# Low parts of the down projection's weights: from VectorE to ScalarE and an adding transfer

## The chip, the core and the metric

The kernel runs on one core of one Trainium2 chip. The metric is the device time of one execution in microseconds; runs of the same kernel are compared by their median.

## The reference, cut to what matters

One layer of a decoder with two token mixers (a gated delta rule and a retention) side by side, a gated sum of the two, an output projection, and then a SwiGLU block, all in float32, for 256 tokens of width 2048. What the change touches is the last product of the SwiGLU block:

```python
hn = rmsnorm(h, norm2_w[l])
h = h + (jax.nn.silu(hn @ w_gate[l]) * (hn @ w_up[l])) @ w_down[l]
return rmsnorm(h, norm_f_w)
```

`w_down` is 5632 x 2048 (46.1 MB).

## The kernel before

Each float32 product is made of three passes on TensorE with operands in a rounded float32 form: the high part of the weights times the high and the low part of the tokens, and the low part of the weights times the high part of the tokens. The kernel works through a row of **units** of weights of up to 1 MB. For each unit, SyncE's queue loads the weights from HBM into a buffer `raw` (`fetch_next`, line 150). ScalarE rounds them to the high part `hi` (line 163), VectorE subtracts, `lo = raw - hi` (line 164), and TensorE makes the passes: in `feature_major` the two with `hi` first (lines 229 and 230, alternating), the one with `lo` last (line 232).

The second phase (its products begin at 819.9 us) has its own buffers beside the shared ones: four for `raw`, three each for `hi` and `lo`. Units are loaded up to three ahead and split up to two ahead of the products (`AHEAD2`, `FETCH`). So a `raw` buffer is filled again when the split of the unit four before has read it, and a `lo` buffer when the products of the unit three before are over.

The inner width of 5632 is cut into four parts of 11 tiles of 128. For each part the gate and up products come first, and then 16 units of the down projection (names `wd0_0` to `wd3_15`; tiles `raw_wd`, `hi_wd`, `lo_wd`, sums `ps_wd`), each 128 x 1408 elements (704 KB) and 33 matrix products of 256 columns. In the first three parts most of the down projection's units alternate with pair units (`sg`, `su`: 512 KB, products in Strassen's form, which have sums of their own on VectorE, lines 181 to 183). In the fourth part the 16 units stand alone, and the kernel ends with them: each sum is added to `hT` (line 1176), squared for the last norm (line 1048) and scaled (line 1181).

The order of instructions on each engine comes from a scheduler that simulates the program with its own durations; in the second phase VectorE keeps the order of the program after the first 30 units. Each engine, and each DMA queue, works strictly in its order.

Of the kernel before, what the change touches and what calls it, by code (L numbers as in the profile page):

```python
# [7 lines left out]
F32 = mybir.dt.float32  # L8
F32R = mybir.dt.float32r
AF = mybir.ActivationFunctionType  # L10
# [10 lines left out]
PAIR = 0        # as a unit's number of columns: a pair of k-tiles for Strassen's products  # L21

# the schedule of the first phase; waits are counted in units of weights
NWARM = 10                      # products that warm the tensor engine up
HOLD, SUMS_AT = 2, 14           # the unit after which the norm of the input, and the sums of it, come
EARLY = 28                      # units up to here may use the banks of Strassen's sums
Q2 = 2                          # pieces of the third unit
SQ = 4                          # pieces of the sum of squares
W_AT0, W_AT, W_TR0, W_TR = 6, 1, 5, 1
PAUSE_M, PAUSE_P = 2, 2         # around the first products of the triangle's inverse  # L30
SP_BEFORE, SP_AFTER = 2, 1      # the units about Strassen's that leave its banks alone
# the token-major blocks of 512 columns (retention v, g, gate_B, z, gate_A) that go through Strassen's products,
# and where: after which unit of their block, among how many units
# [5 lines left out]
# the schedule of the second phase  # L39
MAN0 = 30                       # units after which VectorE keeps the order of the program  # L40
DLY, STEP = 1, 2                # units between products and what reads their sums
# parts of the inner width, in tiles of 128: first, last, and how many groups of 4 go through Strassen's products;
# and where those go: after which unit, among how many
# [5 lines left out]
# buffers; units split ahead in the two phases; units loaded ahead of that  # L49
# [4 lines left out]
# columns of the constants array  # L54
C_ID, C_U, C_L = 0, 128, 256
C_IC = 384                      # compact identity, [128, 32]
C_MK = C_IC + 32                # compact masks of the levels 1 (transposed), 2, 4, 8, 16
# [6 lines left out]
def kernel(  # L64
# [15 lines left out]
    # the banks of Strassen's sums serve the units and the mixers as well while there are none  # L80
# [26 lines left out]
    def find_free():  # L107
        """for each unit, whether it lies clear of Strassen's"""
        pair = [u[1] == PAIR for u in units]
        sp_free[:] = [not any(pair[max(0, i - SP_AFTER):i + SP_BEFORE]) for i in range(len(units))]  # L110
        busy = [i for i, p in enumerate(pair) if p]
        for i in busy:
            if i + 1 < len(units) and any(pair[i + 1:i + 8]):
                for k in range(i, i + 8):
                    sp_free[min(k, len(units) - 1)] = False

    # ---- the work on weights is a row of units of up to 1 MB: load, round to the high part,
    # subtract for the low part, and three passes of products ----
    units = []      # (source, columns, name, compute(hi, lo))
    loaded = []  # L120
    events = {}     # unit number -> what to emit after its products
    done = [0]      # the clock of the events: units done, but for pairs in the first phase
    unit = [0]
    first = [True]  # in the first phase

    more = {}       # tags with one more buffer, in another pool: tag -> (pool, [tiles so far])
# [10 lines left out]
    fetched = []    # units whose load has been emitted  # L137

    def fetch_next(pieces=1):
        """emit the next unit's load, and for a pair its sums; by pieces the split as well"""  # L140
        i = len(fetched)
        src, n, name, _ = units[i]
        raw = wtile("raw", name, F32)
        fetched.append(raw)
        if n == PAIR:
            fetch_pair(src, raw)
            return
        for q in range(pieces):
            r = slice(q * n // pieces, (q + 1) * n // pieces)
            nc.sync.dma_start(raw[:, r], src[:, r])  # L150
            if pieces > 1:
                split_part(i, r)

    parts = []
    split_ins = {}  # unit -> the last instructions of its split, on ScalarE and VectorE

    def split_part(i, r):
# [6 lines left out]
        iv = V.tensor_tensor(out=lo[:, r], in0=w[:, r], in1=hi[:, r].bitcast(F32), op=ALU.subtract)  # L164
        split_ins[i] = ia.ins, iv.ins

    def load_next(pieces=1):
        """emit the next unit's split into high and low parts, and its load if that hasn't been"""
        i = len(loaded)
        if len(fetched) == i:  # L170
            fetch_next(pieces)
        if len(parts) == i:
            split_part(i, slice(0, 1792 if units[i][1] == PAIR else units[i][1]))
        loaded.append(parts[i])

    def fetch_pair(src, raw):
        """a pair of k-tiles by two halves of 256 columns, B12 B11 B22 B21, and the sums of them that
        Strassen's products (in Winograd's form) take: T1 = B12 - B11, -T3 = B12 - B22, T2 = B22 - T1, -T4 = B21 - T2"""
# [6 lines left out]
    def after(n, fn):  # L185
        """emit fn after the products of n more units"""
        events.setdefault(done[0] + n, []).append(fn)

    def chain(gen):
        """emit the steps of gen one by one, one after each unit"""  # L190
# [52 lines left out]
    def start_pair(before):  # L243
        """the first two units, loaded and computed by quarters in turn, each after what `before` emits"""
# [48 lines left out]
    # -- Strassen's products on one block of 512 columns, token-major --  # L293
    def strassen(src, x, zt, name, then, before=None):
# [3 lines left out]
        def lhs(h):  # L298
# [3 lines left out]
            def m(j, i):  # L302
                return (sh if h else sl)[:, j, i]
            # product: its token operand, slot of its weights, bank and half of its sum
            return (
                (lambda j: a(j, 0, 0), 0, 2, 0),      # P1 = A11 B11
                (lambda j: a(j, 1, 0), 2, 0, 0),      # P2 = A12 B21
                (lambda j: a(j, 1, 1), 6, 1, 0),      # -P4 = A22 (-T4)
                (lambda j: m(j, 0), 3, 3, 0),         # P5 = S1 T1
                (lambda j: m(j, 1), 5, 0, 1),         # P6 = S2 T2  # L310
                (lambda j: m(j, 2), 4, 2, 1),         # P7 = S3 T3
                (lambda j: m(j, 3), 1, 1, 1),         # P3 = S4 B22
            )

        def part(j):
            def compute(hi, lo):
                if j == 0:
                    T.extend(ps_sums(f"pst_{name}_{i}") for i in range(4))
                # the first product of a bank marks all of it unwritten
# [14 lines left out]
        def finish():  # L334
            Z, s1 = zt(name)
            A_.activation(s1, T[2][:, 0:S], AF.Copy)
            # slots: C11 U2 U3 U4 C22, then C11 - C21 C12 C22
# [9 lines left out]
    def token_sums(hw, sm, shq, slq):  # L347
        """of two pairs of k-tiles, A11 A21 and A12 A22 (tokens by halves): S1 = A21 + A22,
        S2 = S1 - A11, -S3 = A21 - A11, S4 = A12 - S2"""
# [12 lines left out]
    def spread(main, other, lead=1, tail=0):  # L362
        """other's units evenly among main's, after the first `lead` of them and before the last `tail`"""
# [26 lines left out]
    cosr = cs[:, C_COS:C_COS + S]   # times rstd, once that is known  # L390
    sinr = cs[:, C_SIN:C_SIN + S]

    def rms_scale(ss, r, name):
        """from sums of squares per token, [P, c]: rstd per token, and its broadcast over the partitions in PSUM"""
# [16 lines left out]
    # ================ the projections and the mixers, block by block of two heads ================  # L411
# [38 lines left out]
    def conv_unit(b, i, name, dst, then):  # L450
        """one tile of 128 features: projection, norm, causal conv, silu into dst()."""
# [23 lines left out]
    def new_parts(i):  # L475
        """the merged k-tiles of blocks 2 i and 2 i + 1: high parts, low parts"""
# [14 lines left out]
    def split_rest():  # L491
        """what block 2 has merged, if that came before the last of the sums of u"""
# [25 lines left out]
    def block(b):  # L518
# [3 lines left out]
        def norms(kind, src):  # L522
            """sum of squares + eps and its power -1/2, [P, c, h]; the transposed tiles stay in PSUM."""
# [34 lines left out]
        # -- the triangle of the delta rule and its inverse --  # L558
        def triangle():
# [22 lines left out]
            # blocks of 32 on the diagonal are kept as [P, pair, 32]; MT is the transpose of M  # L582
# [30 lines left out]
            # from blocks of 32 to 64: the lower left block of each is -M22 N21 M11  # L613
# [25 lines left out]
            # from 64 to 128  # L639
# [13 lines left out]
            # -- the outputs of the delta rule --  # L653
# [41 lines left out]
            # q's factor (ss+eps)^-1/2 dk^-1/2 is left out of the output and put back into its norm  # L695
# [55 lines left out]
        # -- retention --  # L751
# [60 lines left out]
        # -- gates, merge, and the transposed split for the output projection --  # L812
        left = [4]      # gates to come
# [138 lines left out]
    def decay():  # L952
        V.tensor_tensor(out=wabs, in0=wabs, in1=w1s.unsqueeze(2).to_broadcast([P, KT, 32]), op=ALU.mult)
        pabT = ps_mix("pabT")
        # k-tiles by fours, each in its own columns of the array; 32 columns each, of which 16 are filled
# [63 lines left out]
    with tc.tile_pool(name="ffn", bufs=1) as ffn:  # L1019
# [22 lines left out]
        def add_square(acc, src, f, name):  # L1042
            """the sums of squares over the k-tiles but the last, whose squares the products add"""
# [162 lines left out]
        def down(pi):  # L1206
            k0, k1, _ = PARTS[pi]
            for f in range(KT):
                # the part's operands are looked up when the unit runs
# [141 lines left out]
```

## Time and profile before

| | |
|---|---|
| median of 3 runs | 1666.42 us (1665.67 to 1667.9) |
| span of the profiled execution | 1664.6 us |
| TensorE | busy 1640.4 us (99%) |
| VectorE | busy 1267.8 us (76%) |
| ScalarE | busy 808.6 us (49%) |
| GpSimd | busy 28.7 us (2%) |
| DMA queue of SyncE | 295.31 MB, 51.4% of 16 engines |

The span runs from the first to the last instruction of one profiled execution; the median is of other runs and lies 1.8 us above it. Busy times of TensorE are of overlapping instructions: one matrix product is given 281 ns, while they start 118 ns apart.

### The profile page before, as it was taken

The numbers are of one execution on the slowest core, as the hardware profiler recorded it, in microseconds if no ns is written. First come the engines' busy times: TensorE is split into PE (matmuls) and PEld (weight loads), VectorE is DVE, ScalarE is ACT, GpSimd is POOL, SyncE is SP. The second block draws the span as 40 slices with busy tenths as digits, with TensorE's granted clock in tenths as the row PEclk, the third lists the DMA queues.
The fourth block names the chain that finished last, engine by engine and source line by source line (L and its number), as shares of the span: only waits on it lengthen the run. The fifth ranks groups of instructions, "written<-read, shape, count | busy, mean of one in ns | idle before, by whom it ended". The sixth has DMA issues, their size and how long they took to land.

```text
span 1664.6 us, 30825 instructions
## 1 busy us (share of the span) xinstructions
PE 1640.4 (99%) x13210; PEld 1558.5 (94%) x13210; DVE 1267.8 (76%) x1719; ACT 808.6 (49%) x850; POOL 28.7 (2%) x63
## 2 busy tenths in 40 slices
PE   7999999999999999999999999999999999999997
PEld 6987899988998889988899999999999999999997
DVE  7797468887888878776675757788778888788754
ACT  5664444445544545445465434444444445354443
POOL 0000000000000000000000000000000000000000
PEclk9999999999999999999999999999999999999998
DMA  7544453454635555344675445465545656466552
GB/s 268 177 153 174 155 194 127 168 185 170 213 131 179 185 180 194 132 168 157 232 270 182 178 152 178 146 219 203 193 170 183 205 190 226 143 205 212 177 181 86
DMA packets 55721, 301.36 MB, mean 181 GB/s; under 512 B 6816, under 2 KB 7072, under 8 KB 32672
## 3 DMA queue, kind: packets, MB, share of 16 engines
q1 hardware_dynamic: 54144, 295.31, 51.4%
q10 hardware_dynamic: 1440, 4.08, 0.7%
q8 instruction: 103, 1.69, 0.4%
q14 instruction: 34, 0.28, 0.0%
HBM read 297.27 MB, written 2.10 MB: 180 GB/s over the span
## 4 chain that ended last, share of the span: by engine, by line
PE 52%; issue 44%; DMA 2%; DVE 2%; ACT 0%; SPq 0%; POOLq 0%; POOL 0%; DVEq 0%; ACTq 0%
PE ps_t L280 7%; PE ps_t L285 7%; PE ps_t L281 7%; PE pst_t L322 6%; PE ps_v L230 2%; PE ps_v L229 2%; PE ps_r L229 2%; PE ps_v L232 2%; PE ps_r L230 2%; PE ps_r L232 2%; PE ps_wo L229 2%; PE ps_wo L230 2%; PE ps_wo L232 1%; PE ps_q L232 1%; PE ps_q L230 1%
## 5 line engine op out<-in xcount | busy, mean ns | idle before, releaser
L163 ACT ACTIVATE hi_t<-raw_t 128x2048 fp32r<-128x2048 f32 (+1 forms) x100 | 183.1, 1832 | 203.7 <-PE ps_t L281 99.2
L164 DVE TENSOR_TENSOR lo_t<-raw_t,hi_t 128x2048 fp32r<-128x2048 f32 (+1 forms) x100 | 217.8, 2182 | 62.4 <-ACT hi_t L163 42.4
L280 PE MATMUL ps_t<-hi_t,uh 128*128 128x512 f32 x480 | 190.7, 397 | 0.5 <-DVE gs L834 0.5
L281 PE MATMUL ps_t<-hi_t,ul 128*128 128x512 f32 x480 | 188.6, 393 | 0.0
L229 PE MATMUL ps_wd<-fh,hi_wd 128*128 128x256 f32 x704 | 169.3, 281 | 1.0 <-DVE fl L1143 1.0
L230 PE MATMUL ps_wd<-fl,hi_wd 128*128 128x256 f32 x704 | 169.6, 281 | 0.0
L229 PEld LDWEIGHTS ps_wd<-fh,hi_wd 128*128 128x128 f32 x704 | 132.8, 189 | 1.2 <-DVE fl L1143 1.2
L230 PEld LDWEIGHTS ps_wd<-fl,hi_wd 128*128 128x128 f32 x704 | 132.9, 189 | 0.0
L163 ACT ACTIVATE hi_wd<-raw_wd 128x1408 fp32r<-128x1408 f32 x64 | 88.4, 1381 | 86.7 <-PE ps_wd L230 35.0
L285 PE MATMUL ps_t<-lo_t,uh 128*128 128x512 f32 x480 | 123.5, 395 | 0.0
L229 PE MATMUL ps_wu<-hh,hi_wu 128*128 128x256 f32 x448 | 109.2, 282 | 0.0
L230 PE MATMUL ps_wu<-hl,hi_wu 128*128 128x256 f32 x448 | 109.1, 283 | 0.0
L230 PE MATMUL ps_wg<-hl,hi_wg 128*128 128x256 f32 x448 | 108.9, 283 | 0.0
L229 PE MATMUL ps_wg<-hh,hi_wg 128*128 128x256 f32 x448 | 108.9, 282 | 0.0
L164 DVE TENSOR_TENSOR lo_wd<-raw_wd,hi_wd 128x1408 fp32r<-128x1408 f32 x64 | 103.6, 1620 | 6.6 <-ACT hi_wd L163 6.5
L280 PEld LDWEIGHTS ps_t<-hi_t,uh 128*128 128x128 f32 x480 | 90.2, 188 | 19.1 <-PE pst_t L322 0.9
L281 PEld LDWEIGHTS ps_t<-hi_t,ul 128*128 128x128 f32 x480 | 90.2, 188 | 17.7
L285 PEld LDWEIGHTS ps_t<-lo_t,uh 128*128 128x128 f32 x480 | 88.9, 188 | 18.1
L232 PE MATMUL ps_wd<-fh,lo_wd 128*128 128x256 f32 x704 | 93.6, 281 | 0.0
L163 ACT ACTIVATE hi_sg<-raw_sg 128x1792 fp32r<-128x1792 f32 x32 | 54.5, 1704 | 71.9 <-DVE raw_sg L183 24.1
L232 PEld LDWEIGHTS ps_wd<-fh,lo_wd 128*128 128x128 f32 x704 | 87.8, 189 | 0.0
L229 PEld LDWEIGHTS ps_wg<-hh,hi_wg 128*128 128x128 f32 x448 | 85.4, 191 | 0.0
(361 smaller groups left out, 4092.1 us busy)
## 6 DMA issues: line engine op xcount, KB each, us to landing
raw_t<-in_wtm_dram SPq DMA_DIRECT2D x60, 1024.0 KB, 4.8
raw_wd<-in_wdown_dram SPq DMA_DIRECT2D x64, 704.0 KB, 4.1
raw_wg<-in_wgate_dram SPq DMA_DIRECT2D x28, 1024.0 KB, 4.8
raw_wu<-in_wup_dram SPq DMA_DIRECT2D x28, 1024.0 KB, 4.8
raw_t<-in_wsm_dram SPq DMA_DIRECT2D x40, 512.0 KB, 3.3
raw_v<-in_wqk_dram SPq DMA_DIRECT2D x16, 1024.0 KB, 4.7
raw_r<-in_wqk_dram SPq DMA_DIRECT2D x16, 1024.0 KB, 4.8
raw_wo<-in_wout_dram SPq DMA_DIRECT2D x16, 1024.0 KB, 4.8
```

The costliest lines, as they stand in the source:

```text
L163: ia = A_.activation(hi[:, r], w[:, r], AF.Copy)
L164: iv = V.tensor_tensor(out=lo[:, r], in0=w[:, r], in1=hi[:, r].bitcast(F32), op=ALU.subtract)
L229: PE.matmul(o[0], hi[:, k * P:(k + 1) * P], ah[:, k, :], start=(k == 0), stop=False)
L230: PE.matmul(o[0], hi[:, k * P:(k + 1) * P], al[:, k, :], start=False, stop=False)
L232: PE.matmul(o[0], lo[:, k * P:(k + 1) * P], ah[:, k, :], start=False, stop=(k == nk - 1))
L280: PE.matmul(pst[c], uh[:, k, c * P:(c + 1) * P], w, start=(k == 0), stop=False)
L281: PE.matmul(pst[c], ul[:, k, c * P:(c + 1) * P], w, start=False, stop=False)
L285: PE.matmul(pst[c], uh[:, k, c * P:(c + 1) * P], lo[:, j * 512:(j + 1) * 512], start=False, stop=(k == KT - 1))
L322: PE.matmul(T[bank][:, half * S:(half + 1) * S], op(j), w[:, slot * 256:(slot + 1) * 256], start=(j == 0 and w is hi and h and half == 0), ...
```

## The change

For the units whose name begins with `wd`, and for no others, VectorE's subtraction is gone. ScalarE writes the rounded high part as before, and then from the same weights a second time, with scale -1 and the same rounding, into `lo`; after that a transfer from SBUF to SBUF, issued from GpSimd's queue, adds `raw` to what stands in `lo`. The rest of the diff drops comments, which moves line numbers by up to 7.

```diff
+LO_BY_DMA = ("wd",)
...
         ia = A_.activation(hi[:, r], w[:, r], AF.Copy)
-        iv = V.tensor_tensor(out=lo[:, r], in0=w[:, r], in1=hi[:, r].bitcast(F32), op=ALU.subtract)
+        if name.startswith(LO_BY_DMA):
+            iv = A_.activation(lo[:, r], w[:, r], AF.Copy, scale=-1.0)
+            G.dma_start(lo[:, r], w[:, r], accum_op=ALU.add)
+        else:
+            iv = V.tensor_tensor(out=lo[:, r], in0=w[:, r], in1=hi[:, r].bitcast(F32), op=ALU.subtract)
         split_ins[i] = ia.ins, iv.ins
```

There are 64 such units, so 64 instructions leave VectorE (line 164), 64 come to ScalarE (line 168 of the changed kernel) and 64 transfers of 704 KB to GpSimd's queue (line 169). Nothing stands otherwise on any engine ahead of the first of them.

GpSimd, last part. The queue before, from its last instructions of the second mixer to the end:

```order
L803 TENSOR_TENSOR gr_7706<-gv_7704,mhalf 128x4
L703 TENSOR_TENSOR fp_8021<-fo_8015,mhalf 128x4
L397 TENSOR_TENSOR rt_8323<-rms_n_9439,mhalf 128x2
L397 TENSOR_TENSOR rtf<-rms_nf,mhalf 128x2
L1346 UNCONDITIONAL_BRANCH
L1346 ISA
```

and the end of it with the change:

```order
L169 DMA lo_wd_11_17266<-raw_wd_11_17217 128x1408
L169 DMA lo_wd_12_17312<-raw_wd_12_17263 128x1408
L169 DMA lo_wd_13_17358<-raw_wd_13_17309 128x1408
L169 DMA lo_wd_14_17404<-raw_wd_14_17355 128x1408
L169 DMA lo_wd_15_17448<-raw_wd_15_17401 128x1408
L404 TENSOR_TENSOR rtf<-rms_nf,mhalf 128x2
L1353 UNCONDITIONAL_BRANCH
L1353 ISA
```

GpSimd had nothing between the second norm and the last; now it issues the 64 transfers there, and the power for the last norm (`rtf`) stands behind them.

ScalarE, last part, around unit 9. Before:

```order
L163 ACTIVATE hi_wd_9_17116<-raw_wd_9_17069 128x1408
L1048 ACTIVATE s_wd_17110<-hT 128x256
L1181 ACTIVATE hT<-hT,wfs 128x256
L163 ACTIVATE hi_wd_10_17161<-raw_wd_10_17114 128x1408
L1048 ACTIVATE s_wd_17155<-hT 128x256
L1181 ACTIVATE hT<-hT,wfs 128x256
L163 ACTIVATE hi_wd_11_17206<-raw_wd_11_17159 128x1408
```

With the change:

```order
L166 ACTIVATE hi_wd_9_17173<-raw_wd_9_17125 128x1408
L1188 ACTIVATE hT<-hT,wfs 128x256
L168 ACTIVATE lo_wd_9_17174<-raw_wd_9_17125 128x1408
L1055 ACTIVATE s_wd_17213<-hT 128x256
L166 ACTIVATE hi_wd_10_17219<-raw_wd_10_17171 128x1408
L1188 ACTIVATE hT<-hT,wfs 128x256
L168 ACTIVATE lo_wd_10_17220<-raw_wd_10_17171 128x1408
L1055 ACTIVATE s_wd_17259<-hT 128x256
L1188 ACTIVATE hT<-hT,wfs 128x256
```

The negated copy (`lo_wd`, line 168) is one instruction more to each unit, behind the rounding of the same unit; the squares and scalings of older sums stand around it.

TensorE, last part, around the pass of unit 9 with the low part. Before (lines 229, 230, 232):

```order
L230 MATMUL ps_wd_9_17210<-fl_16410,hi_wd_9_17116 128x256
L229 MATMUL ps_wd_9_17210<-fh_16409,hi_wd_9_17116 128x256
L230 MATMUL ps_wd_9_17210<-fl_16410,hi_wd_9_17116 128x256
L232 MATMUL ps_wd_9_17210<-fh_16409,lo_wd_9_17117 128x256 x11
L229 MATMUL ps_wd_10_17255<-fh_16409,hi_wd_10_17161 128x256
L230 MATMUL ps_wd_10_17255<-fl_16410,hi_wd_10_17161 128x256
L229 MATMUL ps_wd_10_17255<-fh_16409,hi_wd_10_17161 128x256
```

With the change (the same as lines 236, 237, 239):

```order
L236 MATMUL ps_wd_10_17316<-fh_16457,hi_wd_10_17219 128x256
L237 MATMUL ps_wd_10_17316<-fl_16458,hi_wd_10_17219 128x256
L236 MATMUL ps_wd_11_17362<-fh_16457,hi_wd_11_17265 128x256
L237 MATMUL ps_wd_11_17362<-fl_16458,hi_wd_11_17265 128x256
L239 MATMUL ps_wd_9_17270<-fh_16457,lo_wd_9_17174 128x256 x11
L236 MATMUL ps_wd_11_17362<-fh_16457,hi_wd_11_17265 128x256
L237 MATMUL ps_wd_11_17362<-fl_16458,hi_wd_11_17265 128x256
```

and the end of the products with the change:

```order
L237 MATMUL ps_wd_15_17530<-fl_16458,hi_wd_15_17447 128x256
L236 MATMUL ps_wd_15_17530<-fh_16457,hi_wd_15_17447 128x256
L237 MATMUL ps_wd_15_17530<-fl_16458,hi_wd_15_17447 128x256
L239 MATMUL ps_wd_14_17491<-fh_16457,lo_wd_14_17404 128x256 x11
L239 MATMUL ps_wd_15_17530<-fh_16457,lo_wd_15_17448 128x256 x11
L1065 MATMUL ss_nf<-ones,acc_16938 128x1 x2
L1065 MATMUL ss_nf<-ones,s_wd_17570 128x1 x2
```

The pass with the low part of unit 9 no longer ends unit 9: it is made after all 22 products of unit 10 and the first two of unit 11. The last two such passes stand back to back at the end. In the first three parts these passes are moved back likewise, by up to one unit.

## Rows read from the trace of the kernel before

**Rows 1.** The page, part 1: busy us, share of the span, instructions of each engine.
```profile
span 1664.6 us, 30825 instructions
...
PE 1640.4 (99%) x13210; PEld 1558.5 (94%) x13210; DVE 1267.8 (76%) x1719; ACT 808.6 (49%) x850; POOL 28.7 (2%) x63
```

**Rows 2.** Stretches of down projection: length, busy time, granted clock, DMA share, GB/s.
```profile
core 0: us, PE busy (x) PEld busy (x) DVE busy (x) ACT busy (x) POOL busy (x), PEclk, DMA share, GB/s
1050.00:1146.00 96.00, 96.00 (x813) 96.00 (x812) 81.36 (x95) 45.19 (x34) 0.00 (x0) 1.00 0.61 192
1254.00:1354.00 100.00, 100.00 (x847) 100.00 (x845) 85.29 (x100) 48.45 (x35) 0.00 (x0) 1.00 0.60 195
1450.00:1546.00 96.00, 96.00 (x813) 96.00 (x812) 82.05 (x94) 46.94 (x34) 0.00 (x0) 1.00 0.66 210
1577.00:1652.00 75.00, 73.81 (x624) 73.49 (x622) 42.95 (x58) 35.69 (x51) 0.00 (x0) 1.00 0.39 126
```

**Rows 3.** Waits of TensorE, 1040 to 1660 us: total, times, longest.
```profile
PE rb_nf L402 <- DVE dg_nf L401: 1.3, 1, 1.3
PE ps_wd L229 <- DVE fl L1143: 1.0, 1, 1.0
PE ss_nf L1058 <- ACT s_wd L1048: 0.6, 1, 0.6
```

**Rows 4.** The same stretches, instructions that touch lo_wd alone.
```profile
sum 367.00, PE 93.58 PEld 87.78 DVE 103.57; mean PE 23.40 PEld 21.94 DVE 25.89
```

**Rows 5.** ScalarE in mid last part, 1600 to 1640 us: count, busy, mean, idle before.
```profile
L163 ACT ACTIVATE hi_wd<-raw_wd 128x1408 fp32r<-128x1408 f32 x11 | 15.2, 1381 | 16.6 <-PE ps_wd L230 16.6
L1181 ACT ACTIVATE hT<-hT,wfs 128x256 f32<-128x256 f32 x11 | 5.6, 509 | 0.3
L1048 ACT ACTIVATE s_wd<-hT 128x256 f32<-128x256 f32 x11 | 4.4, 401 | 0.0
```

**Rows 6.** VectorE in order of time, last part, two units.
```profile
1613.28 1.62 DVE L164 TENSOR_TENSOR lo_wd<-raw_wd,hi_wd 128x1408 fp32r<-128x1408 f32 x1
1614.82 0.42 DVE L1176 TENSOR_TENSOR hT<-ps_wd,hT 128x256 f32<-128x256 f32 x1
...
1617.15 1.62 DVE L164 TENSOR_TENSOR lo_wd<-raw_wd,hi_wd 128x1408 fp32r<-128x1408 f32 x1
1618.69 0.42 DVE L1176 TENSOR_TENSOR hT<-ps_wd,hT 128x256 f32<-128x256 f32 x1
```

**Rows 7.** DMA, 1040 to 1660 us: queue (packets, MB, share), issues (KB each, us to landing).
```profile
q1 hardware_dynamic: 22847, 112.35, 54.5%
...
raw_wd<-in_wdown_dram SPq DMA_DIRECT2D x63, 704.0 KB, 4.1
...
raw_su<-in_wst_dram SPq DMA_DIRECT2D x32, 512.0 KB, 3.6
```

**Rows 8.** DMA, 1600 to 1640 us, in 40 slices of 1 us.
```profile
DMA  8959669179507943692379246923690000000000
GB/s 293 394 214 372 124 231 400 39 141 383 214 0 130 389 203 45 141 422 113 45 197 406 81 51 197 406 84 62 203 428 28 0 0 0 0 0 0 0 0 16
```

**Rows 9.** DMA issues, before 1042 us: the slowest large load.
```profile
hT<-in_xT_dram ACTq DMA_DIRECT2D x2, 1024.0 KB, 13.2
```

**Rows 10.** GpSimd, whole run: count, busy, mean ns, idle before.
```profile
L397 POOL TENSOR_TENSOR rstd_t<-rms_n,mhalf 128x2 f32<-128x2 f32 x1 | 2.7, 2677 | 30.3 <-DVE rms_n L396 30.3
```

**Rows 11.** Instructions that touch raw_wd, SyncE queue: ns min/median/max, first and last start.
```profile
L150 SPq DMA_DIRECT2D raw_wd<-in_wdown_dram x64: 327/328/328, 1034.3 to 1626.7; - x64
```

## The prediction

> **What bounds the kernel now.** Start with the page's first part: TensorE is busy for 1640.4 of 1664.6 us, VectorE for 76%, ScalarE for 49% [rows 1]. The busy share alone doesn't settle it, since the products overlap; so look at the pace next. I cut the second phase into the four stretches in which the down projection's units are split and multiplied, one for each part of the inner width: 96, 100, 96 and 75 us long [rows 2]. In each TensorE starts a product every 118 ns (96.00 us by 813; 73.81 us by 624), at a granted clock of 1.00. A pace that is the same in mixed and in pure stretches, with VectorE busy 85% in one and 57% in the other, is TensorE's own. Then the waits: from 1040 to 1660 us TensorE waited 1.0 us for VectorE among the down projection's products, and 1.9 us in the last norm, behind all of them [rows 3]. So TensorE bounds, and what the change takes off VectorE was hidden.
>
> What is not far from a bound is the third view, the DMA share: 0.61, 0.60, 0.66 and 0.39 of the 16 engines in the four stretches [rows 2]. That is what the change puts weight on.
>
> **What the change removes.** 64 subtractions, 103.57 us of VectorE's time, all inside the stretches [rows 4]. They are worth at most the 1.0 us that TensorE waited for VectorE there [rows 3], and that wait was for the low part of the tokens, not of the weights. I count 0 and keep -1.0 us.
>
> **What it adds on ScalarE.** 64 negated copies, priced by the rounding of the same shape, 1.38 us [rows 5]: 88 us in all. The tightest place is the last part, where a unit comes every 3.87 us (from 1613.28 to 1617.15) [rows 6]. There ScalarE does the rounding, the scaling and the square, 1.38 + 0.51 + 0.40 = 2.29 us; the rest of each unit it waits for TensorE to free the buffer [rows 5]. With 1.38 more it has 3.67 us of work in 3.87. That fits, with 0.2 us to spare, so 0; without the cover it would cost 1.38 us a unit.
>
> **What it adds on GpSimd's queue.** 64 issues. Ahead of them the queue is empty in this phase; behind the last stands only the power for the last norm, which waits for TensorE's last products anyway. What an issue with an addition costs GpSimd no row shows: the bounds are 0.33 us, which SyncE takes for one of its 64 issues of `raw_wd` [rows 11], and 2.7 us, the slowest GpSimd instruction [rows 10]. Either is less than a unit, so it only adds to the delay.
>
> **What it adds on the DMA engines.** This is the term that decides. No transfer within SBUF, and no adding one, is in the trace. What 704 KB cost once through comes from the loads: 112.35 MB in 54.5% of 620 us, 337.9 us of all 16 engines, is 332 GB/s, so 720,896 bytes take 2.17 us [rows 7]. In its best slice a load moved 428 GB/s, which makes 1.68 us [rows 8]. The adding transfer writes 704 KB too, but must read two tiles of 704 KB, `raw` and the old `lo`. If an engine's time goes by what it reads, the price is double: 3.4 us at the best pace, 4.3 us at the mean one. I take 3.4: nothing here waits for HBM, as in the slices where a load ran unbroken. The other ends: 1.7 us, if the second read is free; and 9.1 us, from the slowest load, 1024 KB in 13.2 us, scaled to 704 KB [rows 9].
>
> The Trainium skill has a rule that speaks against this change: "Collectives: The Full Stack", section "The bandwidth ceiling: the fold count and why AG ≠ RS ≠ AR", says that an addition inside the DMA engines isn't slow because of the adding, but because it needs two source reads on one ring, and reports 62.28 against 32.35 GB/s, a ratio of 1.93. No row here shows an addition. By that ratio on the mean price of a load the transfer would cost 4.2 us as an estimate, and the sum below would be some 112 us instead of 62.
>
> Now the sum by stretch. The loads use length times share: 58.6, 60.0, 63.4 and 29.3 us [rows 2]. Each stretch gets 16 transfers, 54.4 us at 3.4. Together that is 113.0, 114.4, 117.8 and 83.7 us of all engines, in stretches of 96, 100, 96 and 75 us: 17.0, 14.4, 21.8 and 8.7 us too much, 62 us in all. It cannot be moved elsewhere, as loads run only three units ahead and a transfer only two. The point of break-even is where 16 transfers fit beside the loads: 2.3, 2.5, 2.0 and 2.9 us for one in the four stretches.
>
> **What then waits.** TensorE's order is made for some delay: the pass with the low part is moved back by about a unit, so in the changed order it stands some 100 products, 12 us, behind the pass that frees its buffer. A turn of a `lo` buffer is the copy 1.4, the issue up to 2.7, the start and end of a transfer 1.9 (a load of 2.17 lands after 4.1 [rows 7]), the transfer 3.4 and the pass 1.3 (11 products), at most 10.7 us for three units of 3.87, 11.6 us. With a load of 2.2 us between its packets it is 12.9, a little beyond. So the throughput fails first, and the delay is close behind it; I add nothing for it. As the backlog grows, the first to be late is TensorE's pass with `lo_wd`, and with it everything in its order. SyncE's queue is next: a load now waits until the transfer has read the `raw` buffer, and behind it stand the loads of the pair units, 3.6 us each [rows 7], and of the next part's gate and up weights. ScalarE's negated copy waits for the old `lo` to be used up, with the next unit's rounding behind it.
>
> **The sum.** 1664.6 + 62 = 1726.6 us for the profiled execution; the median of the runs stood 1.8 us above it. I predict 1728 us.
>
> **Rivals.** (1) The transfer is hidden. If the second read goes on beside the first, a transfer costs 1.7 to 2.2 us, 27 to 35 us in a stretch, and fits everywhere but in the third (98 in 96 us). The time is then 1666 to 1669 us. For it: the share is of busy engines, and two queues may fill gaps that one leaves; in 1-us slices the loads swing between 0.9 and 0 [rows 8]. If both kinds went at the 428 GB/s of the best slice, loads and doubled transfers together would nearly fit as well: the third stretch, 210 GB/s by 96 us, is 20.2 MB or 47 us, and with 54 us of transfers 101 in 96. Against: packets of both queues share the same engines, and the mean of 332 GB/s is what SyncE's long run of loads got. It decides where one transfer falls under 2.0 us.
>
> (2) Faster than before. It needs TensorE to wait for VectorE's low parts, in places that the subtractions' going makes early. The only such wait is 1.0 us [rows 3], so the end is 1665 us, inside the noise; to win 3.3 us, 0.2%, which is about what a measurement of this kernel can tell from no change, there would have to be three times as much. It decides only if the transfers are hidden too.
>
> (3) The addition itself is slow. At 5.4 us a transfer, about two and a half loads at the mean price, the four stretches are 49, 46, 54 and 41 us over, 190 in all: 1856 us. At 9.1 us it is 427 over, 2093 us. For it: an addition has to hold the first read until the second comes, which no load does. Against: only the one slow pair of loads [rows 9], which shared the engines with SyncE's own.
>
> (4) The change doesn't do what it says: VectorE keeps the subtractions. The orders of instructions rule that out, so no chance is given.
>
> **How the numbers follow.** Two reads at 3.4 to 4.3 us (1728 to 1786 us; 4.3 us is 16 by 4.3 = 69 us a stretch, 31, 29, 36 and 23 over, 119 in all), with the cases shading down to 2.5 us: 0.60. Hidden: 0.17, of which 0.12 within 0.2% and 0.05 a little above. Faster: 0.03. Slow addition: 0.20, half of it under 1870 us. So slower by over 0.2%: 0.85, the same 0.12, faster 0.03. The range goes from 1667, a hidden transfer, up to 1870, some way into the third rival; the likeliest case alone runs from 1700 to 1790.
>
> **What would show it.** VectorE loses 64 instructions and some 104 us, ScalarE gains 64 of 1.38 us. The DMA share in the four stretches rises to 0.9 or more, and the stretches grow by about 17, 14, 22 and 9 us, the third most and the fourth least. TensorE, without waits before, waits ahead of the passes on line 239 for GpSimd's transfers. SyncE's loads of `raw_wd` land later than after 4.1 us. All before 1040 us stays as it is. I am wrong if the DMA share stays near 0.8 while TensorE waits (then it is delay or GpSimd's issue, not throughput), if the fourth stretch, with the lowest share, grows most (then a price for each transfer in turn bounds it, whatever the loads do), or if TensorE doesn't wait at all. A granted clock under 1.00 in the stretches would be a cost that the sum leaves out.

## The result, and the profile after

The changed kernel takes 1774.42 us (median of 4 runs, 1769.72 to 1776.44), the kernel before 1666.53 us beside it: a ratio of 1.0642, with a 95% interval of 1.0627 to 1.0657, or 107.9 us more. The forecast was 1728 us, with a range of 1667 to 1870.

The page of the changed kernel, part 1 (as [rows 1]):

```profile
span 1774.7 us, 30995 instructions
...
PE 1680.3 (95%) x13210; PEld 1587.7 (89%) x13210; DVE 1170.8 (66%) x1655; ACT 886.5 (50%) x914; POOL 84.8 (5%) x127
```

VectorE lost 64 instructions and 97 us, ScalarE gained 64 and 78 us, and GpSimd, which had 28.7 us of work, has 84.8. TensorE makes the same 13210 products, in 40 us more of busy time, and is no longer busy throughout.

**Where the time went.** The stretches of [rows 2] can't be laid over the new trace, as everything in it comes later. A mark that both programs have is VectorE's product `us` of the last gate and up unit of each part, just ahead of that part's down projection. VectorE's timeline, the kernel before:

```profile
1054.60 0.42 DVE L1167 TENSOR_TENSOR us<-us,gs 128x256 f32<-128x256 f32 x1
...
1257.64 0.42 DVE L1167 TENSOR_TENSOR us<-us,gs 128x256 f32<-128x256 f32 x1
...
1453.96 0.43 DVE L1167 TENSOR_TENSOR us<-us,gs 128x256 f32<-128x256 f32 x1
...
1591.03 0.42 DVE L1167 TENSOR_TENSOR us<-us,gs 128x256 f32<-128x256 f32 x1
```

The same marks in the changed kernel:

```profile
1054.56 0.42 DVE L1174 TENSOR_TENSOR us<-us,gs 128x256 f32<-128x256 f32 x1
...
1290.07 0.43 DVE L1174 TENSOR_TENSOR us<-us,gs 128x256 f32<-128x256 f32 x1
...
1517.20 0.43 DVE L1174 TENSOR_TENSOR us<-us,gs 128x256 f32<-128x256 f32 x1
...
1681.68 0.43 DVE L1174 TENSOR_TENSOR us<-us,gs 128x256 f32<-128x256 f32 x1
```

The first mark stands where it stood: nothing changed ahead of it. From mark to mark, and from the last one to the end of the span, the four parts grew by 32.5, 30.8, 27.4 and 19.5 us. (A part is the down projection together with the next part's gate and up units.) These four numbers are worked out in the same way for the other kernels below, each from its profiled execution.

The stretches of the down projection in the changed kernel, columns as in [rows 2]:

```profile
core 0: us, PE busy (x) PEld busy (x) DVE busy (x) ACT busy (x) POOL busy (x), PEclk, DMA share, GB/s
1054.56:1200.62 146.06, 125.42 (x973) 122.62 (x973) 70.43 (x92) 72.63 (x55) 13.08 (x15) 0.94 0.82 223
1290.07:1437.69 147.62, 126.87 (x965) 124.30 (x964) 73.71 (x95) 74.30 (x57) 13.08 (x15) 0.91 0.84 229
1517.20:1653.73 136.53, 119.16 (x943) 116.52 (x942) 68.43 (x88) 71.38 (x54) 13.08 (x15) 0.96 0.89 246
1681.68:1761.00 79.32, 67.74 (x522) 65.58 (x522) 13.21 (x32) 46.13 (x57) 11.36 (x13) 0.95 0.91 224
```

The DMA share, 0.39 to 0.66 before, is 0.82 to 0.91, and TensorE stands idle for 12 to 21 us in each stretch. What it waits for, 1040 to 1770 us (as [rows 3]: total, times, longest):

```profile
PE ps_wd L239 <- DMA lo_wd<-raw_wd: 31.2, 24, 4.7
PE ps_wd L236 <- ACT hi_wd L166: 29.9, 12, 5.5
PE pst_su L329 <- ACT hi_su L166: 5.2, 6, 1.4
PE ps_wd L236 <- DVE hT L1183: 3.4, 1, 3.4
```

Only the first row is the pass with the low part, late because of its transfer. The second is as large: the rounded high part came late, and no transfer stands between it and the load. Two rows of SyncE's waits between the same times say why (line 187 issues the loads of the pair units, line 153 all the other loads of weights, those of the down projection among them):

```profile
SPq L153 <- DMA lo_wd<-raw_wd: 211.8, 40, 10.7
SPq L187 <- DMA lo_wd<-raw_wd: 108.7, 18, 10.4
```

58 loads were issued when an adding transfer had ended, because that transfer still read the `raw` buffer that they were to fill. In the kernel before, 50 loads waited likewise for VectorE's subtraction (1040 to 1660 us; lines 150 and 180 are its lines of these loads), but for less than half as long in all:

```profile
SPq L150 <- DVE lo_wd L164: 101.0, 31, 9.4
SPq L180 <- DVE lo_wd L164: 52.1, 19, 6.7
```

So it isn't new that a load waits for its buffer; what is new is how late the buffer comes free. The profile's chain of work that ended last shows this loop turning (start, length, what):

```profile
1521.50 3.40 issue
...
1524.92 10.10 DMA lo_wd<-raw_wd
...
1535.03 10.63 DMA raw_wd<-in_wdown_dram
...
1545.72 2.97 issue
...
1548.70 3.40 DMA lo_wd<-raw_wd
```

A load lands, ScalarE makes its two copies (the 3 us of "issue"), GpSimd issues, the transfer takes 10.1 us, and only then does the next load start.

The DMA view, 1040 to 1770 us (as [rows 7]):

```profile
q1 hardware_dynamic: 22877, 112.35, 43.4%
q0 software_dynamic: 9216, 46.14, 33.5%
...
lo_wd<-raw_wd POOLq DMA_DIRECT2D x64, 704.0 KB, 7.3
raw_wd<-in_wdown_dram SPq DMA_DIRECT2D x63, 704.0 KB, 6.4
```

GpSimd's transfers are the queue q0: 33.5% of 730 us by 64 is 3.82 us of all 16 engines for one transfer, and a load that landed after 4.1 us [rows 7] now takes 6.4.

### The profile page after: what moved, and what is told of

It is laid out like the page before. It is cut to its first block, busy times and chain, and to the rows that moved or that the text cites. A ratio compares the mean times of both kernels' runs of the same rounds, so it can differ in the third digit from the quotient of the medians.

```text
span 1774.7 us, 30995 instructions
## 1 busy us (share of the span) xinstructions
PE 1680.3 (95%) x13210; PEld 1587.7 (89%) x13210; DVE 1170.8 (66%) x1655; ACT 886.5 (50%) x914; POOL 84.8 (5%) x127
## 4 chain that ended last, share of the span: by engine, by line
PE 72%; DMA 18%; issue 6%; DVE 2%; ACT 2%; SPq 0%; POOL 0%; POOLq 0%; DVEq 0%; ACTq 0%
DMA lo_wd<-raw_wd 9%; DMA raw_wd<-in_wdown_dram 7%; PE ps_t L287 6%; PE ps_t L292 6%; PE ps_t L288 6%; PE pst_t L329 5%; PE ps_wg L239 3%; PE ps_wu L239 3%; PE ps_wu L237 3%; PE ps_wu L236 3%; PE ps_wg L236 3%; PE ps_wg L237 3%; PE pst_sg L329 2%; PE pst_su L329 2%; PE ps_v L237 2%
## 5 line engine op out<-in xcount | busy, mean ns | idle before, releaser
L236 PE MATMUL ps_wd<-fh,hi_wd 128*128 128x256 f32 x704 | 183.9, 297 | 35.1 <-ACT hi_wd L166 29.9
L237 PE MATMUL ps_wd<-fl,hi_wd 128*128 128x256 f32 x704 | 182.1, 294 | 0.0
L236 PEld LDWEIGHTS ps_wd<-fh,hi_wd 128*128 128x128 f32 x704 | 142.8, 203 | 38.6 <-ACT hi_wd L166 32.6
L237 PEld LDWEIGHTS ps_wd<-fl,hi_wd 128*128 128x128 f32 x704 | 143.0, 203 | 0.0
L239 PE MATMUL ps_wd<-fh,lo_wd 128*128 128x256 f32 x704 | 105.6, 303 | 31.2 <-DMA lo_wd<-raw_wd 31.2
L239 PEld LDWEIGHTS ps_wd<-fh,lo_wd 128*128 128x128 f32 x704 | 96.5, 207 | 36.3 <-DMA lo_wd<-raw_wd 36.1
L287 PEld LDWEIGHTS ps_t<-hi_t,uh 128*128 128x128 f32 x480 | 90.2, 188 | 19.1 <-PE pst_t L329 0.9
L171 DVE TENSOR_TENSOR lo_sg<-raw_sg,hi_sg 128x1792 fp32r<-128x1792 f32 x32 | 64.8, 2024 | 53.4 <-PE ps_wd L239 25.3
L168 ACT ACTIVATE lo_wd<-raw_wd 128x1408 fp32r<-128x1408 f32 x64 | 87.3, 1368 | 22.8 <-PE ps_wd L239 18.7
L171 DVE TENSOR_TENSOR lo_su<-raw_su,hi_su 128x1792 fp32r<-128x1792 f32 x32 | 64.7, 2022 | 45.0 <-ACT hi_su L166 41.0
```

Source lines behind the costliest of these rows:

```text
L168: iv = A_.activation(lo[:, r], w[:, r], AF.Copy, scale=-1.0)
L236: PE.matmul(o[0], hi[:, k * P:(k + 1) * P], ah[:, k, :], start=(k == 0), stop=False)
L237: PE.matmul(o[0], hi[:, k * P:(k + 1) * P], al[:, k, :], start=False, stop=False)
L239: PE.matmul(o[0], lo[:, k * P:(k + 1) * P], ah[:, k, :], start=False, stop=(k == nk - 1))
L287: PE.matmul(pst[c], uh[:, k, c * P:(c + 1) * P], w, start=(k == 0), stop=False)
```

## The experiments

Two theories were to be told apart. Throughput: the transfers and the loads together need more time of the 16 engines than the stretches have. Delay: a transfer lasts so long, and holds its buffers so long, that the rings of buffers turn too slowly, whatever the engines could carry. Diffs are against the changed kernel.

**ScalarE's copies alone** (`neg_only`).

```diff
-            G.dma_start(lo[:, r], w[:, r], accum_op=ALU.add)
```

> ScalarE writes the negated copy into lo, and no transfer adds anything to it; lo is minus the high part. Throughput theory (the adding transfers and the loads together ask for more of the 16 DMA engines than there is): without transfers nothing is left, 1666 us, within 3 us of before. Rival (ScalarE's second copy is what holds the units up, as it has 3.67 us of work in 3.87 us of a unit in the last part): at least a third of the 108 us stays, over 1700 us.

Measured: 1668.77 us, 2.2 us over the kernel before, ratio 1.0014 (1.0004 to 1.0023). ScalarE's copies, the subtractions that VectorE no longer makes and the new order of instructions cost nearly nothing together; the rest comes with the transfers.

**One read in place of two** (`copy_only`).

```diff
-            G.dma_start(lo[:, r], w[:, r], accum_op=ALU.add)
+            G.dma_start(lo[:, r], w[:, r])
```

> The same 64 transfers with the same order and waits, but a plain copy of raw into lo, so one read in place of two; the last pass multiplies the whole weights. Throughput theory with two reads: a transfer falls from the 3.83 us of 16 engines measured in the changed kernel to about 1.9, 30 us in a stretch, which fits beside the loads: 1666 to 1675 us. Rival (delay: each transfer's start, end and issue, and the queues behind it): only about 2 of 7.3 us from issue to landing go, so half or more of the loss stays, 1715 us or more.

Measured: 1698.19 us, 31.6 over, ratio 1.019 (1.0175 to 1.0205). Its DMA view, 1040 to 1700 us:

```profile
q0 software_dynamic: 9216, 46.14, 19.1%
...
lo_wd<-raw_wd POOLq DMA_DIRECT2D x64, 704.0 KB, 5.1
```

The same packets and bytes take 1.97 us of the engines each (19.1% of 660 us by 64), 1.94 times less than with the addition. (Whether the second read doubles the time or the adding itself, no run separates; below, "second read" stands for the addition with all that belongs to it.) The parts grew by 16.9, 7.9, 3.7 and 1.4 us. By the prediction's sum, with 31.5 us of transfers beside the loads of [rows 2], this fits into every stretch (90 in 96, 92 in 100, 95 in 96, 61 in 75), and yet it costs some 30 us. The time lies between the two expectations.

**Transfers that the products don't wait for** (`unawaited`). VectorE subtracts as before; ScalarE and the adding transfers fill columns of `lo` and `hi` that nobody reads, 640 KB a unit.

```diff
-            iv = A_.activation(lo[:, r], w[:, r], AF.Copy, scale=-1.0)
-            G.dma_start(lo[:, r], w[:, r], accum_op=ALU.add)
+            iv = V.tensor_tensor(out=lo[:, r], in0=w[:, r], in1=hi[:, r].bitcast(F32), op=ALU.subtract)
+            for k, x in enumerate((lo, hi)):
+                A_.activation(x[:, 1408:2048], w[:, 640 * k:640 * k + 640], AF.Copy, scale=-1.0)
+                G.dma_start(x[:, 1408:2048], w[:, 640 * k:640 * k + 640], accum_op=ALU.add)
```

> VectorE subtracts as before, so no product waits for a transfer. Beside it ScalarE writes two negated pieces of 640 columns into the unused columns of the hi and lo buffers and two transfers add the weights to them: 91% of the bytes of the change, in 128 transfers, awaited only when a buffer is written again. Throughput theory: the loads are held up as in the change; 16 times 3.5 us in a stretch make about 65 to 90 us over, 1730 to 1760 us. Rival (delay of the transfer ahead of the pass with the low part): nearly all is gone, under 1690 us.

Measured: 1761.05 us, 94.5 over, ratio 1.0575 (1.0558 to 1.0593), a little above what throughput alone was to give. What TensorE waits for, 1040 to 1760 us:

```profile
PE ps_wd L238 <- ACT hi_wd L166: 33.6, 14, 4.8
PE ps_wd L241 <- DVE lo_wd L168: 15.8, 12, 3.3
```

No product waits for a transfer directly, and the loss is nearly whole. So a late pass with the low part isn't needed for it; the loads are late, by busy engines, by held buffers, or by both. (In this kernel the transfers write into `hi` as well as `lo`, so they hold those buffers too.)

**The last part alone** (`last_part`).

```diff
-LO_BY_DMA = ("wd",)
+LO_BY_DMA = ("wd3",)
```

> The change for the last 16 of the 64 units alone. The last part added 13.4 us of the 109.3 in the changed kernel's trace. Throughput theory: the stretches are separate, so 13 us, 1679 us, against 15.6 by the sum at 3.83 us a transfer. Rival (the loss carries over from one part to the next, through a TensorE clock that stays low or loads that stay late): less than 8 us here, under 1674 us.

Measured: 1683.75 us, 17.2 over, ratio 1.0105 (1.0089 to 1.012); the last part grew by 17.8 us. By the marks above it had grown by 19.5 us in the whole change (the 13.4 us that the expectation names do not come out of these marks), so it owes at most a small part of that to a backlog from the parts ahead. Both numbers lie 2 to 4 us above the 15.6 us that the sum gives.

**The weights from HBM, so that the transfer doesn't hold `raw`** (`from_hbm`).

```diff
-            G.dma_start(lo[:, r], w[:, r], accum_op=ALU.add)
+            G.dma_start(lo[:, r], units[i][0][:, r], accum_op=ALU.add)
```

> The adding transfer takes the weights from HBM a second time in place of the raw buffer, so a raw buffer is free as soon as ScalarE has read it twice; the engines read and write as many bytes. Ring theory (beside the engines' throughput, the turn of four raw buffers is too long: load, two copies, issue, transfer, and the next load into the buffer waits for the transfer): the part of the 110 us that the sum at 3.83 us a transfer leaves open, some 20 us, goes, and the first two parts gain most: about 1755 us. Throughput alone: the same within 8 us of 1774, or slower if reads from HBM are dearer.

Measured: 1754.14 us, 87.4 over, ratio 1.0522 (1.05 to 1.0543). The waits of TensorE, 1040 to 1770 us:

```profile
PE ps_wd L239 <- DMA lo_wd<-in_wdown_dram: 49.3, 38, 4.2
PE ps_wd L236 <- ACT hi_wd L166: 5.2, 4, 2.2
```

and of SyncE's queue:

```profile
SPq L153 <- ACT lo_wd L168: 150.9, 32, 11.7
```

The wait for `hi_wd` falls from 29.9 to 5.2 us, since a load now starts when ScalarE has read the buffer; the transfers are later than before, and 20.5 us of the 107.9 are won back, as the theory of the ring had it. By part 9.6, 4.5, 7.6 and 1.6 us are won, so the second part did not gain as much as was expected of it. Not all need be the buffer: a transfer takes 3.70 us of the engines here instead of 3.82 (32.4% of 730 us by 64).

**Three buffers for `raw` instead of four** (`raw3`, and the kernel before with the same edit, `before_raw3`).

```diff
-        for tag in WBUFS:
+        for tag in ("hi", "lo"):
```

> The change with three raw buffers in place of four in the second phase. Ring theory: the turn is shared by three buffers, so the mixed parts get clearly slower, 20 us or more over the changed kernel beyond what the same step costs the kernel before. Throughput alone: the engines have the same work, within 8 us of 1774 plus what the same step costs the kernel before.

> The kernel before with three raw buffers in the second phase, the control for the run above. Loads of 4.1 us and a split of some 3 us make a turn of 7 us for three units of 2.5 to 3.9 us, which fits: within 8 us of 1666 by both theories.

Measured: 1845.62 us with the change, 178.9 over and 71.0 more than with four buffers, ratio 1.1072 (1.1048 to 1.1096); 1666.55 us without the change, ratio 1.0 (0.999 to 1.001). The kernel before has no use for the fourth buffer; the changed one needs it. The DMA view of the changed one, 1040 to 1850 us:

```profile
q1 hardware_dynamic: 23549, 113.93, 41.3%
q0 software_dynamic: 9216, 46.14, 29.9%
```

The engines are less busy than in the changed kernel (71% against 77%) while the time is longer: the 71.0 us are not engines that had more to carry.

**Three buffers, weights from HBM** (`from_hbm_raw3`: both edits above).

> The transfer takes its weights from HBM, with three raw buffers in place of four. Ring theory: a raw buffer is no longer held by the transfer, so the third buffer less costs little, as in the kernel before: 1754 us, within 10. If the 71 us of the run with three buffers came from fewer loads in flight beside saturated engines, they come back here: over 1790 us.

Measured: 1783.85 us, 117.4 over, ratio 1.0696 (1.0662 to 1.073); 30.0 more than with four buffers, between the two expectations. So of the 71.0 us about 41 go when the transfer no longer holds the buffer. The other 30 may come from having one load fewer under way while the engines are busy, but that isn't shown, because here too a load waits for work of the change on its buffer, ScalarE's second reading (SyncE's waits, 1040 to 1790 us):

```profile
SPq L187 <- ACT lo_wd L168: 68.7, 18, 11.6
SPq L153 <- ACT lo_wd L168: 58.5, 22, 10.1
```

**A plain copy from HBM** (`copy_hbm`: neither the second read nor a held buffer).

```diff
-            G.dma_start(lo[:, r], w[:, r], accum_op=ALU.add)
+            G.dma_start(lo[:, r], units[i][0][:, r])
```

> The plain copy of the second run, with the weights taken from HBM in place of the raw buffer; the last pass multiplies the whole weights. If the throughput of two reads and the holding of the raw buffers are the two causes, both are taken away: 1666 to 1675 us, against 1698 with the copy from the raw buffer. If what stayed with the plain copy is the delay ahead of the pass with the low part (three lo buffers), it stays here too: 1690 us or more.

Measured: 1682.08 us, 15.6 over, ratio 1.0096 (1.0079 to 1.0113), again in between. With this the four corners are there, in us over the kernel before:

| | weights from `raw` | weights from HBM |
|---|---|---|
| addition (two reads) | 107.9 | 87.4 |
| plain copy (one read) | 31.6 | 15.6 |

The second read is worth 76.3 or 71.8 us, the held buffer 20.5 or 16.0: the two depend little on each other.

**Half of each transfer, and every second transfer** (`half_cols`, `every_2nd`).

```diff
-            iv = A_.activation(lo[:, r], w[:, r], AF.Copy, scale=-1.0)
-            G.dma_start(lo[:, r], w[:, r], accum_op=ALU.add)
+            c = 704
+            A_.activation(lo[:, 0:c], w[:, 0:c], AF.Copy, scale=-1.0)
+            G.dma_start(lo[:, 0:c], w[:, 0:c], accum_op=ALU.add)
+            iv = V.tensor_tensor(out=lo[:, c:1408], in0=w[:, c:1408], in1=hi[:, c:1408].bitcast(F32), op=ALU.subtract)
```

```diff
-        if name.startswith(LO_BY_DMA):
+        if name.startswith(LO_BY_DMA) and int(name.split("_")[1]) % 2:
```

> ScalarE's negated copy and the transfer make 704 of the 1408 columns of each low part, VectorE subtracts the other 704; 64 transfers of half the size. Throughput: 31 us in a stretch as in the run above, which fits: 1666 to 1675 us. Ring of raw buffers: the turn is about as long as with the plain copies (1.97 us of the engines for one), so about the same 30 us stay: 1690 to 1700 us.

> The change for every second of the 16 units of a part, VectorE's subtraction for the others. Throughput: 8 transfers of 3.83 us are 31 us in a stretch, which fits beside the loads everywhere (89, 91, 94 and 60 us in 96, 100, 96 and 75): 1666 to 1675 us. Ring of raw buffers: only half of the turns are long, some 10 to 20 us left: 1676 to 1686 us.

Measured: 1693.7 us, 27.3 over, ratio 1.0164 (1.0149 to 1.0179), for the halves; 1706.42 us, 40.0 over, ratio 1.024 (1.0217 to 1.0262), for every second one, more than either theory allowed. The same bytes in fewer and longer transfers cost more. In the profiled executions (1695.22 and 1701.84 us) the parts grew by 13.6, 8.8, 7.1 and -0.1 us with the halves, by 14.4, 7.9, 9.9 and 3.9 with every second one. A stretch of the first and of the fourth part, halves:

```profile
1050.00:1175.00 125.00, 115.87 (x942) 114.64 (x941) 83.10 (x110) 64.11 (x55) 13.35 (x16) 0.97 0.78 216
...
1620.00:1680.00 60.00, 59.64 (x505) 59.44 (x504) 24.03 (x45) 40.05 (x57) 11.34 (x13) 1.00 0.84 212
```

and of every second one:

```profile
1050.00:1175.00 125.00, 115.35 (x934) 113.94 (x934) 79.39 (x100) 61.91 (x48) 7.14 (x8) 0.97 0.72 216
...
1620.00:1687.00 67.00, 63.10 (x530) 62.70 (x530) 25.62 (x43) 38.88 (x53) 6.09 (x7) 1.00 0.74 195
```

With the halves the last part runs at a DMA share of 0.84 and TensorE is idle for 0.4 us of 60; the first runs at 0.78 and TensorE is idle for 9 of 125. A mean share doesn't tell whether a stretch loses time.

**More work for TensorE** (`filler`: eight products with a weight of zero ahead of each pass with the low part, 512 in all).

```diff
+            if zero and name.startswith(LO_BY_DMA):
+                for k in range(8):
+                    PE.matmul(o[0], zero[0], ah[:, k, :], start=False, stop=False)
...
+        zero.append(ffn.tile([P, P], F32R, name="zero"))
+        A_.activation(zero[0], w2s[:, 0:1].to_broadcast([P, P]), AF.Copy, scale=0.0)
```

> The change with 8 more products with zero weights ahead of each pass with the low part, 64 times 0.94 us, 60 us of TensorE's work. If the transfers set the pace and the products that run at the lower clock only fill waits: less than 20 us more, 1775 to 1795 us. If the lower clock (40 us more of TensorE's busy time) is itself on the path, TensorE is still the bound: most of the 60 us are added, 1815 us or more, unless the zero products keep the clock up, and then the time falls under 1765.

Measured: 1783.4 us, 116.7 over the kernel before and 8.8 over the change, ratio 1.0711 (1.0681 to 1.0741). The page:

```profile
PE 1719.4 (97%) x13722; PEld 1633.1 (92%) x13722; DVE 1171.3 (66%) x1655; ACT 889.4 (50%) x915; POOL 84.8 (5%) x127
```

512 products are 60 us at 118 ns [rows 2], and 51 of these 60 us vanish in time that TensorE had been waiting or slow; the mean granted clock rose from 0.976 to 0.987. TensorE no longer sets the pace.

## Why the prediction was right or wrong

**Right: the direction, the bound and the way.** What left VectorE and what came to ScalarE cost 2.2 us together, against the 0 of the sum. 108 us came through the DMA engines, TensorE's wait ahead of line 239 appeared, and the time lies in the likeliest case's own range of 1700 to 1790. The first rival is out: one transfer costs 3.82 us. So is the third: it needed 5.4. But the sum had only 62 of the 108 us; two steps of it fell short.

**Mis-sized: "I take 3.4".** The price was taken as twice the best pace of a load, because nothing waits for HBM. It came out at 3.82 us, between that and the 4.3 of the mean pace. The factor itself held: 3.82 by the copy's 1.97 is 1.94. The Trainium skill's "Collectives: The Full Stack", section "The bandwidth ceiling: the fold count and why AG ≠ RS ≠ AR", reports a ratio of 1.93 between a collective that only copies and one that adds, and puts it down to two source reads. This case's ratio of 1.94 agrees with it, for transfers of a single core. Put into the prediction's sum, the measured price, 61.1 us of transfers in a stretch instead of 54.4, gives 23.7, 21.1, 28.5 and 15.4 us, 89 in all. That is close to what the kernel loses whose transfers don't hold `raw`, 87.4 us, but partly by luck: by that kernel's own price of 3.70 us the sum is 81, its parts grew by 22.9, 26.3, 19.8 and 17.9 us, where the sum has the third as the largest, and for the copies from HBM the same sum gives next to nothing where 15.6 us were measured. In the last part alone, throughput is plain. The DMA view of the changed kernel, 1700 to 1740 us:

```profile
q0 software_dynamic: 1017, 5.08, 63.2%
q1 hardware_dynamic: 1096, 5.50, 38.6%
```

The two queues together fill the engines there (they come to 102%, as a packet counts whole where it starts), and with one read or half the columns the same part loses 1.4 us or nothing.

**Failed: "the throughput fails first, and the delay is close behind it; I add nothing for it".** The prediction worked out the turn of a `lo` buffer, and for `raw` it only said that a load would wait; it counted no turn there. Estimated from the medians of the changed kernel, with the loads already late: load 6.4, two copies 2.7, transfer 7.3 with its issue in it, 16.4 us in all. Four buffers cover the products of four units: 15.5 us where the units stand alone (3.87 each, [rows 6]), and some 12.7 in the mixed parts, where every second unit is a pair unit of about 21 products, 2.5 us. Even with the prediction's own terms, 4.1, 2.8 and 5.3 for the transfer, it is 12.2 us before any issue of GpSimd's, at the edge. This loop is what SyncE's waits and the wait for `hi_wd` show, and letting go of `raw` wins 20.5 us with the addition and 16.0 with the copies.

**Failed: the break-even price.** The prediction let a transfer be hidden below 2.0 to 2.9 us. The copies of 1.97 us cost 31.6, and half of the adding work cost 27 to 40 us, though the sums fit. So the first rival fails twice: the price isn't what it took, and at its price the transfers would not have been hidden. The likely reason, argued and not shown by a run of its own: loads and transfers come in bunches that a sum over 96 us doesn't see, and where a long transfer meets a load, the load lands late.

**Half right: the pattern of the stretches.** "The third most and the fourth least" and a share of "0.9 or more" were to show it. The fourth did grow least, but the first grew most and the third only third, and the share was 0.82 and 0.84 in the first two parts, near the mark at which the prediction itself wanted delay instead of throughput. In the mixed parts both are at work: letting go of `raw` won 4.5 to 9.6 us in each. In the pure last part, where it won 1.6 of 19.5 us, it is throughput.

**The clock.** The prediction left it out of the sum, and said that it would be a cost if it fell. TensorE's granted clock fell below 1.00 in the stretches in which it waits. Between 1140 and 1160 us, where it was idle for a quarter of the time, the mean was 0.83. Three slices of 1 us show the two levels, 2.4 GHz (1.00) and 1.2 GHz (0.50), columns as in [rows 2]:

```profile
1149.00:1150.00 1.00, 0.00 (x0) 0.00 (x0) 0.00 (x0) 0.00 (x0) 0.00 (x0) 1.00 1.02 422
1152.00:1153.00 1.00, 1.00 (x7) 1.00 (x6) 0.00 (x0) 1.00 (x2) 0.04 (x1) 0.50 0.45 180
1158.00:1159.00 1.00, 1.00 (x11) 1.00 (x10) 0.68 (x2) 0.68 (x1) 0.00 (x0) 1.00 0.74 146
```

It fell while TensorE stood idle and rose again while it worked. The 40 us of longer busy time lie mostly in the waits' shadow: the filler brought the clock up, and 60 us more of products cost 9. That the low clock costs nothing isn't shown, as no run took it away without adding work.

**What stays open.** The plain copy from HBM still costs 15.6 us, of which ScalarE's copies explain 2.2. In its trace TensorE is busy for 6.2 us longer than before and idle for 8.9 us longer, of which 4.5 are ahead of the pass with the low part (1040 to 1680 us):

```profile
PE ps_wd L239 <- DMA lo_wd<-in_wdown_dram: 4.5, 4, 2.3
```

What sets the rest wasn't tried. How the 72 to 76 us of the addition divide in the mixed parts, between engines without time and turns that a longer transfer makes longer, no run separates. Nor is it shown why the first part loses most in every kernel with four buffers in which `raw` is held.

## What to carry to other kernels

An addition inside a transfer cost the DMA engines 1.94 times a copy here: price it at twice a copy, and add it to the loads' time stretch by stretch. Then walk around the ring of every buffer that the transfer reads or writes, not only the one that it fills: the source is held until the transfer has ended, and the sum of load, copies, issue and landing, under load, must be below the work that the ring's buffers cover. A sum that fits at 92 to 99% of the engines isn't hidden: the copies from `raw` cost 4 to 17 us in each such stretch. In the last part, with copies or halves at 81 or 82% of its length (61 of 75 us), at most 2.2 us were lost, though every second transfer, at 80%, cost 3.9.

## What the runs showed of the hardware

GpSimd needs longer to issue an adding transfer than a plain one. GpSimd's instructions by line, the changed kernel:

```profile
L169 POOL DMA_DIRECT2D lo_wd<-raw_wd x64 | 56.0, 875 | 776.3 <-ACT lo_wd L168 390.3 <-ACT sg L1164 129.9 <-DVE gs L1162 120.0
```

and with the plain copy:

```profile
L169 POOL DMA_DIRECT2D lo_wd<-raw_wd x64 | 34.7, 543 | 720.7 <-ACT lo_wd L168 380.5 <-ACT sg L1164 129.9 <-DVE gs L1162 120.9
```

That is 875 against 543 ns for one. An adding transfer of half the columns takes 876 ns (`half_cols`), so the time did not go by the bytes. The adding transfer lands 7.3 us after its issue in the median, the copy after 5.1, and halving an adding transfer brings its landing only to 6.5 us while its price on the engines halves to 2.01 (19.5% of 660 us by 64): so between half and two thirds of a landing is not the transfer's own time on the engines. How much of the rest is waiting among other packets, and how much the start and end of a transfer, wasn't measured. Where the source is HBM instead of SBUF, the price is about the same (3.70 against 3.82 us with the addition, 1.95 against 1.97 without), and the landing later (10.4 and 6.5 us).
